# A hybrid decoder layer on one core: the first norm's squares in blocks of four, its factor applied per row block, small constants and two modulation chunks loaded later

## The chip, the cores and the metric

The kernel runs on one core of a Trainium2 chip. The metric is device time in microseconds (us) of one execution; of before there are three runs with a median of 1945.05 us (1939.61 to 1948.28). A separate profiled execution took 1943.4 us, and its trace spans 1941.6 us.

## The reference, cut to what matters

One layer over 256 tokens of width 2048, in float32: an adaLN modulation, a norm, one input projection for attention (NSA) and retention, an output projection, then a second norm with a retrieval among 16384 experts, and a last norm. The change touches only the start:

```python
c_act = jax.nn.silu(c)
mod = (c_act @ w_ada[l] + b_ada[l]).reshape(B, 6, 1, D)
shift1, scale1, gate1, shift2, scale2, gate2 = jnp.moveaxis(mod, 1, 0)
h = rmsnorm(x, g_norm_mix[l]) * (1.0 + scale1) + shift1
q_a, k_c, v_c, k_s, v_s, k_w, v_w, g_a, q_r, k_r, v_r, g_r = split_cols(h @ w_in[l], IN_SIZES)
```

`rmsnorm` divides each token by the root of its mean square (plus 1e-6) and multiplies by a gain per feature.

## The kernel before, in words

Features lie on partitions in 16 row blocks of 128, tokens (256) along the free axis: `xT` is 128x16x256. Weights arrive in chunks of 128x2048 f32 (1.05 MB) through a ring of four `raw` tiles, by SP's queue, in program order. A weight chunk is split in two parts, `whi` by a cast on ACT (L156) and `wlo` by a subtraction on DVE (L157); each has two tiles. TensorE multiplies them with the two parts `hh` and `hl` of the normed input (together the tile `act`), in three products (hi with hh, hi with hl, lo with hh).

The modulation w_ada is 96 chunks `adaT` (j, k): part j of six, row block k. Each is one multiply-and-sum over 128x2048 on DVE (L197) against silu(c), the tile `crow`. The first 32, shift (j = 0) and scale (j = 1), are needed by row blocks 0 to 15; the others are worked off in the background until the output projection. The function `background` takes as many as a pace per stage says, and `row_in(k)` first takes those that row block k needs. The stages at the front are

- the norm: 16 squares on ACT (L249), a running sum on DVE (L253), a sum over partitions by TensorE, the power -0.5 on POOL (`pow_mhalf`, L219), a diagonal and a matmul that spread it as a row (`rrow`), and four multiplications of `xT` by it (L298);
- A: row blocks 0 to 7 of the input, 2048 columns, 16 column blocks in 8 PSUM banks `bkA`. Per row block: load and split `winA`, scale and shift `xT` (L293), cast it (`hh`, L294), subtract (`hl`, L295), two background chunks, then 48 matmuls;
- C: the same row blocks, 1024 further columns, 4 chunks, banks `bkC`;
- B: all 16 row blocks, 1664 columns, banks `bkB`, `bvB`, `bgB`; row blocks 8 to 15 are modulated here. In this text "row 14" and "row 15" are its last two;
- D and NSA: 12 chunks `winD` over row blocks 8 to 15 (`psD`), mixed with the attention. D0 is the first of them, D1 the second. The compressed keys need `kT2`, which four POOL DMAs turn from `kcv`, and tables `nal` (16 of 192 KB, four tiles) and `csm`, `small`.

A list scheduler puts the instructions of each engine in order by program position, so the order on an engine is not the order in the code. An engine runs its list strictly in that order.

Of the kernel before, what the change touches and what calls it, by code (L numbers as in the profile page):

```python
# [20 lines left out]
P = 128  # L21
# [93 lines left out]
def body(ctx, tc, a, out, dbg=None, stop=None):  # L115
# [130 lines left out]

    def sumsq(wpool, kb, acc, src, tag="pr"):
        sq = wpool.tile([P, S], F32, name="sq", tag=tag, bufs=3)
        nc.scalar.activation(sq, src, AF.Square)  # L249
        if kb == 0:  # L250
            nc.vector.tensor_copy(acc, sq)
        else:
            nc.vector.tensor_add(acc, acc, sq)  # L253

    def row_rstd(pool, wpool, accs, tags, ident, copy=True):

        ps = [pool.tile([P, 2], F32, name="psq", tag=t) for t in tags]
        for i, acc in enumerate(accs):
            for tt in range(2):
                nc.tensor.matmul(ps[tt][:, 0:1], acc[:, tt * P:(tt + 1) * P], ones[:, 0:1], start=i == 0, stop=i == len(accs) - 1)  # L260
        rc = wpool.tile([P, 2], F32, name="rcol")
        for tt in range(2):
            nc.vector.tensor_scalar(rc[:, tt:tt + 1], ps[tt][:, 0:1], 1.0 / D, EPS, op0=OP.mult, op1=OP.add)
        pow_mhalf(rc, rc, 2)
        dg = wpool.tile([P, S], F32, name="rdiag", tag="pr", bufs=3)
        for tt in range(2):
            nc.vector.tensor_scalar(dg[:, tt * P:(tt + 1) * P], ident, rc[:, tt:tt + 1], None, op0=OP.mult)
        ps = pool.tile([P, S], F32, name="psr", tag=tags[0])
        nc.tensor.matmul(ps, ones, dg, start=True, stop=True)
        if not copy:  # L270
            return ps
        r = wpool.tile([P, S], F32, name="rrow")
        nc.scalar.copy(r, ps)
        return r


    with ExitStack() as fctx:
# [3 lines left out]
        nc.vector.memset(ones, 1.0)  # L281
        small = fp.tile([P, 128 + 480 + 30], F32, name="small")
        nc.gpsimd.dma_start(small, a["small"][:, 0:638])
        ident = small[:, 0:128]
        ncmp = small[:, 128:608].rearrange("p (t h n) -> p t h n", t=2, h=HEADS)
        cval = small[:, 608:638].rearrange("p (t n) -> p t n", t=2)
        csm = fp.tile([P, 160], F32, name="csm")
        nc.gpsimd.dma_start(csm, a["csm"])

        def modulate(k, e, t, gi, sh, hh, hl):  # L290

            for i in range(k, e):
                nc.scalar.activation(t[:, i - k, :], t[:, i - k, :], AF.Identity, bias=modc[:, sh, i:i + 1], scale=scol[:, gi, i:i + 1])  # L293
            nc.scalar.copy(hh[:, k:e, :], t)  # L294
            nc.vector.tensor_sub(hl[:, k:e, :], t, hh[:, k:e, :].bitcast(F32))  # L295

        def normalise(dst, src, rrow):
            nc.vector.tensor_mul(dst, src, rrow[:, None, :].to_broadcast([P, dst.shape[1], S]))  # L298

# [8 lines left out]
        pp = fctx.enter_context(tc.tile_pool(name="fpsum", bufs=2, space=PS))  # L308
        banks = lambda name, shape, tags: [pp.tile(shape, F32, name=f"{name}{i}", tag=t) for i, t in enumerate(tags)]
        crow = c_row(fp, pp)  # L310
        for q in range(4):
            nc.sync.dma_start(xT[:, 4 * q:4 * q + 4, :], a["xT"][:, 4 * q:4 * q + 4, :])
        acc = fp.tile([P, S], F32, name="sqacc")
        for k in range(KB):
            sumsq(fp, k, acc, xT[:, k, :])
        rrow = row_rstd(pp, fp, [acc], ["S", "S"], ident)
        for k in range(0, KB, 4):
            normalise(xT[:, k:k + 4, :], xT[:, k:k + 4, :], rrow)

# [4 lines left out]
        def background(n=1):  # L324
            credit[0] += PACE[n] if isinstance(n, str) else n
            n = int(credit[0] + 1e-6)
            credit[0] -= n
            for _ in range(n):
                if not todo:
                    return  # L330
                j, k = todo.pop(0)
                ada_chunk(j, k, crow)
                if j == 0:
                    nc.vector.tensor_add(modc[:, 0:2, k], modc[:, 0:2, k], b_col[:, 0:2, k])
                    nc.vector.tensor_scalar(scol[:, 0, k:k + 1], modc[:, 1, k:k + 1], 1.0, g_mix[:, k:k + 1],
                                            op0=OP.add, op1=OP.mult)
# [9 lines left out]

        def rows_T(bank, b, hi, lo, col, k, k0, k1, first=True):
            w = slice(col, col + P)
            for n, (x, y) in enumerate(((hi, hh), (hi, hl), (lo, hh))):
                nc.tensor.matmul(bank[:, b, :], x[:, w], y[:, k, :], start=k == k0 and n == 0 and first,  # L350
# [7 lines left out]
        def row_in(k):  # L358
            while len(todo) > 96 - 2 * (k + 1):
                background(1)  # L360
            modulate(k, k + 1, xT[:, k:k + 1, :], 0, 0, hh, hl)

# [9 lines left out]
        for k in range(KH):  # L372
            hi, lo = win_row(a["winA"], k, 2048)
            row_in(k)
            background("A")
            for b in range(16):
                rows_T(bk[b // 2], b % 2, hi, lo, b * P, k, 0, KH, b % 2 == 0)
        wait_in(oT, bk)
        bk = banks("bkC", [P, 2, S], "AASS")
        for q in range(KH // 2):  # L380
# [134 lines left out]
        for gp in range(2):  # L515
# [3 lines left out]
            for r in range(4):  # L519
# [5 lines left out]
                for hf in range(2):  # L525
# [776 lines left out]
```

## Time and profile before

| what | before |
|---|---|
| median of the runs | 1945.05 us |
| profiled execution, its span | 1943.4 us, 1941.6 us |
| TensorE busy | 1826.8 us, 94% of the span |
| DVE busy | 1479.4 us, 76% |
| DMA | 651.86 MB, mean 336 GB/s |

A share of busy time is a mean over stages with different limits. What a change at the front is worth has to be read from the stretch it touches, and from what TensorE does right behind it.

### The profile page before, as it was taken

To read this page: it belongs to the slowest core of one execution; us is meant where nothing else is said; L and a number is where in the kernel's file an instruction comes from. 1 tells how busy PE (TensorE), PEld (TensorE's weight loads), DVE (VectorE), ACT (ScalarE), POOL (GpSimd) and SP (SyncE) were. 2 spreads that over 40 slices of the span, in tenths; PEclk is the share of its full clock that TensorE was granted. 3 is DMA by queue.
4 is the path that set the end of the run, shared out by engine and by line. 5 is a ranking of instruction groups with operands and counts; after the bars stand their busy time and mean duration, and the time that the engine had idled before them with its cause. 6 is when DMAs were issued, how large, how long until landed. Compare 5 with 4: busy or idle time off the path is not lost.

```text
span 1941.6 us, 28423 instructions
## 1 busy us (share of the span) xinstructions
PE 1826.8 (94%) x11302; PEld 1594.3 (82%) x11302; DVE 1479.4 (76%) x2247; ACT 699.4 (36%) x1192; POOL 348.6 (18%) x254
## 2 busy tenths in 40 slices
PE   5899899999987999989999999999999999999995
PEld 4798778788766899989997767779999998777773
DVE  7877888889985898487578888874455557899875
ACT  3444353635434421021134444451111114555552
POOL 1000001011010012102123323221111212344210
PEclk9999998989988999999999999999999999999998
DMA  8989888989993589989989999989999989999981
GB/s 341 381 310 358 324 303 271 346 287 377 374 321 134 185 297 386 424 319 376 361 357 402 348 382 372 340 307 375 397 357 360 361 303 376 383 394 383 388 323 44
DMA packets 94312, 651.86 MB, mean 336 GB/s; under 512 B 11410, under 2 KB 11586, under 8 KB 18402
## 3 DMA queue, kind: packets, MB, share of 16 engines
q1 hardware_dynamic: 66818, 467.78, 63.6%
q0 software_dynamic: 27360, 182.26, 24.2%
q8 instruction: 89, 1.46, 0.3%
q14 instruction: 45, 0.36, 0.0%
HBM read 643.92 MB, written 4.21 MB: 334 GB/s over the span
## 4 chain that ended last, share of the span: by engine, by line
PE 73%; DVE 11%; DMA 6%; issue 6%; ACT 3%; POOL 0%; SPq 0%; ACTq 0%; POOLq 0%; DVEq 0%
PE acc L960 30%; PE psU L1058 27%; PE psN L449 4%; DVE wlo L157 3%; DMA raw<-in_adaT 2%; DVE raw L197 2%; PE psA L235 2%; PE psD L350 2%; ACT whi L156 2%; PE pg L1043 1%; DMA raw<-in_winA 1%; PE psA L236 1%; PE bkB L350 1%; DMA x2d<-xT 1%; PE bkC L350 1%
## 5 line engine op out<-in xcount | busy, mean ns | idle before, releaser
L157 DVE TENSOR_TENSOR wlo<-raw,whi 128x2048 fp32r<-128x2048 f32 (+2 forms) x215 | 479.3, 2239 | 139.3 <-ACT whi L156 90.0
L1058 PE MATMUL psU<-xT,raw 128*128 128x160 f32 x4096 | 570.8, 301 | 5.8 <-ACT ge L1063 4.5
L1058 PEld LDWEIGHTS psU<-xT,raw 128*128 128x128 f32 x4096 | 560.2, 191 | 6.5 <-ACT ge L1063 4.6
L156 ACT CAST whi<-raw 128x2048 fp32r<-128x2048 f32 (+2 forms) x215 | 400.7, 1869 | 228.0 <-PE psA L235 40.7
L960 PE MATMUL acc<-whi,cc 128*128 128x512 f32 x1512 | 376.3, 396 | 16.7 <-ACT whi L156 16.7
L960 PEld LDWEIGHTS acc<-whi,cc 128*128 128x128 f32 x1512 | 286.6, 190 | 89.4 <-ACT whi L156 19.8
L960 PE MATMUL acc<-wlo,cc 128*128 128x512 f32 x1008 | 257.1, 395 | 2.3 <-DVE wlo L157 2.3
L197 DVE SCALAR_TENSOR_TENSOR raw<-raw,crow 128x2048 f32<-128x2048 f32 x96 | 219.3, 2286 | 21.5 <-DMA raw<-in_adaT 21.4
L960 PEld LDWEIGHTS acc<-wlo,cc 128*128 128x128 f32 x1008 | 164.6, 164 | 66.9 <-DVE wlo L157 5.1
L449 PE MATMUL psN<-whi,act 128*128 128x512 f32 x512 | 166.1, 400 | 2.3 <-ACT sg L628 2.3
L1064 DVE TENSOR_TENSOR X<-X,ge 128x160 f32<-128x160 f32 (+19 forms) x94 | 26.0, 278 | 156.2 <-ACT ge L1063 146.6
L1060 ACT ACTIVATE X<-psU 128x160 f32<-128x160 f32 (+19 forms) x102 | 25.6, 252 | 330.8 <-PE psU L1058 330.7
L449 PEld LDWEIGHTS psN<-whi,act 128*128 128x128 f32 x512 | 95.9, 188 | 25.0 <-ACT sg L628 2.7
L936 ACT CAST cc<-X 128x192 fp32r<-128x192 f32 x128 | 44.8, 353 | 197.1 <-PE acc L960 197.1
L449 PE MATMUL psN<-wlo,act 128*128 128x512 f32 x256 | 103.3, 404 | 3.0 <-DVE wlo L157 2.9
L235 PE MATMUL psA<-act,whi 128*128 128x512 f32 x240 | 87.4, 405 | 8.6 <-ACT whi L156 8.6
L800 POOL DMA_INDIRECT rows<-in_urow,sx x32 | 59.8, 1869 | 130.1 <-DVE rows L841 100.5
L350 PE MATMUL psD<-act,whi 128*128 128x256 f32 x384 | 76.3, 298 | 3.6 <-ACT whi L156 3.6
L800 POOL DMA_INDIRECT xT<-in_v,sx x21 | 57.3, 2727 | 119.6 <-DVE cc L937 76.6
L800 POOL DMA_INDIRECT s<-in_urow,sx x26 | 47.1, 1811 | 145.7 <-DVE s L841 111.6
L841 DVE SCALAR_TENSOR_TENSOR rows<-rows,h2t 128x2048 f32<-128x2048 f32 x32 | 73.0, 2284 | 0.0
L350 PEld LDWEIGHTS psD<-act,whi 128*128 128x128 f32 x384 | 63.2, 201 | 6.4 <-ACT whi L156 4.0
(339 smaller groups left out, 2406.8 us busy)
## 6 DMA issues: line engine op xcount, KB each, us to landing
raw<-in_u SPq DMA_DIRECT2D x128, 1024.0 KB
raw<-in_v SPq DMA_DIRECT2D x128, 1024.0 KB
raw<-in_adaT SPq DMA_DIRECT2D x96, 1024.0 KB
raw<-in_winN SPq DMA_DIRECT2D x16, 1024.0 KB
raw<-in_woutN SPq DMA_DIRECT2D x16, 1024.0 KB
raw<-in_wqT SPq DMA_DIRECT2D x16, 1024.0 KB
raw<-in_winB SPq DMA_DIRECT2D x16, 832.0 KB
raw<-in_winD SPq DMA_DIRECT2D x12, 1024.0 KB
```

The costliest lines, as they stand in the source:

```text
L156: nc.scalar.copy(hi[:, sl], r[:, sl])
L157: nc.vector.tensor_sub(lo[:, sl], r[:, sl], hi[:, sl].bitcast(F32))
L197: nc.vector.scalar_tensor_tensor(r, r, 1.0, crow, op0=OP.mult, op1=OP.mult, accum_out=modc[:, j, k:k + 1])
L235: nc.tensor.matmul(p_, hi[:, sl], act[:, k], start=k == 0, stop=False, skip_group_check=True)
L350: nc.tensor.matmul(bank[:, b, :], x[:, w], y[:, k, :], start=k == k0 and n == 0 and first, stop=k == k1 - 1 and n == 2, skip_group_check=True)
L449: nc.tensor.matmul(ps[tt], x[:, k, ts_], y[:, w], start=k == 0 and j == 0, stop=k == KB - 1 and j == 2)
L800: pin(nc.gpsimd.indirect_dma_start(out=r, out_offset=None, in_=src, in_offset=bass.IndirectOffsetOnAxis(ap=o, axis=0)))
L841: pin(nc.vector.scalar_tensor_tensor(r, r, 1.0, h, op0=OP.mult, op1=OP.mult, accum_out=d[:, e:e + 1]))
L936: nc.scalar.copy(ch, xb(j))
L960: nc.tensor.matmul(acc[c][0:m], x, w[:, c[1] * 512:(c[1] + 1) * 512], start=jj == 0 and n == 0, stop=jj == HALF - 1 and n == 2 - c[0], ski ...
L1058: nc.tensor.matmul(ps, w[:, k * P:(k + 1) * P], xT[:, k, 0:TU], start=k == 0, stop=k == KB - 1)
L1064: nc.vector.tensor_mul(xb(j)[:, 0:done], xb(j)[:, 0:done], ge[:, 0:done])
```

## The change

The squares are taken over four row blocks at once (128x1024), the running sum is folded on DVE in the end, and the 1/D with 1e-6, the diagonal and the copy of the norm move from DVE to ACT; all of this has a raised priority. `xT` is no longer multiplied by `rrow` in four wide steps: per row block one DVE instruction multiplies by scale and `rrow`, ACT adds the shift while it casts to `hh`, and a second DVE instruction makes `hl`. The bias of the shift is added on POOL, one instruction per row block; 1 + b_ada is made once. Only `ident` is loaded at the start; `csm` and the rest of `small` go on SP's queue after stage A's last `winA`, and the `nal` loads of POOL's queue behind the `kT2` turns. In stage A the matmuls run product by product over all 16 column blocks, and the last row block takes no background chunks. B's `bv` and `bg` swap bank tags, and D0's load and split are issued ahead of the copies of B's banks.

```diff
-    def sumsq(wpool, kb, acc, src, tag="pr"):
-    def row_rstd(pool, wpool, accs, tags, ident, copy=True):
...
-        small = fp.tile([P, 128 + 480 + 30], F32, name="small")
-        nc.gpsimd.dma_start(small, a["small"][:, 0:638])
+        ident = fp.tile([P, P], F32, name="ident")
+        nc.gpsimd.dma_start(ident, a["small"][:, 0:128])
...
-        nc.gpsimd.dma_start(csm, a["csm"])
-
-        def modulate(k, e, t, gi, sh, hh, hl):
-
-            for i in range(k, e):
-                nc.scalar.activation(t[:, i - k, :], t[:, i - k, :], AF.Identity, bias=modc[:, sh, i:i + 1], scale=scol[:, gi, i:i + 1])
-            nc.scalar.copy(hh[:, k:e, :], t)
-            nc.vector.tensor_sub(hl[:, k:e, :], t, hh[:, k:e, :].bitcast(F32))
-
-        def normalise(dst, src, rrow):
-            nc.vector.tensor_mul(dst, src, rrow[:, None, :].to_broadcast([P, dst.shape[1], S]))
+        def modulate(k):
+
+            t, shift = xT[:, k, :], modc[:, 0, k:k + 1]
+            nc.vector.scalar_tensor_tensor(t, t, scol[:, 0, k:k + 1], rrow, op0=OP.mult, op1=OP.mult)
+            nc.scalar.activation(hh[:, k, :], t, AF.Identity, bias=shift)
+            nc.vector.scalar_tensor_tensor(hl[:, k, :], t, shift, hh[:, k, :].bitcast(F32), op0=OP.add, op1=OP.subtract)
...
-        acc = fp.tile([P, S], F32, name="sqacc")
-        for k in range(KB):
-            sumsq(fp, k, acc, xT[:, k, :])
-        rrow = row_rstd(pp, fp, [acc], ["S", "S"], ident)
-        for k in range(0, KB, 4):
-            normalise(xT[:, k:k + 4, :], xT[:, k:k + 4, :], rrow)
+        with tc.high_priority(offset=200):
+            for q in range(4):
+                sq = acc if q == 0 else sqs[(q + 1) % 2]
+                nc.scalar.activation(sq, xT[:, 4 * q:4 * q + 4, :], AF.Square)
+                if q in (1, 2):
+                    nc.vector.tensor_add(acc, acc, sq)
+                if q > 1:
+                    fold(acc if q == 2 else sq)
+                    by_token(acc if q == 2 else sq, q == 2)
+            rc = fp.tile([P, 2], F32, name="rcol")
+            for tt in range(2):
+                nc.scalar.activation(rc[:, tt:tt + 1], psq[tt][:, 0:1], AF.Identity, bias=eps, scale=1.0 / D)
+            pow_mhalf(rc, rc, 2)
+            dg = fp.tile([P, S], F32, name="rdiag", tag="pr", bufs=3)
+            for tt in range(2):
+                nc.scalar.activation(dg[:, tt * P:(tt + 1) * P], ident, AF.Copy, scale=rc[:, tt:tt + 1])
+            psr = pp.tile([P, S], F32, name="psr", tag="S")
+            nc.tensor.matmul(psr, ones, dg, start=True, stop=True)
+            nc.scalar.copy(rrow, psr)
...
                 if j == 0:
-                    nc.vector.tensor_add(modc[:, 0:2, k], modc[:, 0:2, k], b_col[:, 0:2, k])
-                    nc.vector.tensor_scalar(scol[:, 0, k:k + 1], modc[:, 1, k:k + 1], 1.0, g_mix[:, k:k + 1],
+                    nc.gpsimd.tensor_add(modc[:, 0, k:k + 1], modc[:, 0, k:k + 1], b_col[:, 0, k:k + 1])
+                elif j == 1:
+                    nc.vector.tensor_scalar(scol[:, 0, k:k + 1], modc[:, 1, k:k + 1], b1[:, k:k + 1], g_mix[:, k:k + 1],
...
             row_in(k)
-            background("A")
-            for b in range(16):
-                rows_T(bk[b // 2], b % 2, hi, lo, b * P, k, 0, KH, b % 2 == 0)
+            if k < KH - 1:
+                background("A")
+            for n in range(3):
+                for b in range(16):
+                    rows_T(bk[b // 2], b % 2, hi, lo, b * P, k, 0, KH, b % 2 == 0, (n,))
         wait_in(oT, bk)
+        for dst, src in ((csm, a["csm"]), (small, a["small"][:, 128:638])):
+            tc.keep_in_program_order(nc.sync.dma_start(dst, src))
...
-        bv = banks("bvB", [P, 512], "AA")
-        bg, = banks("bgB", [P, 1, S], "S")
+        bv = banks("bvB", [P, 512], "SS")
+        bg, = banks("bgB", [P, 1, S], "A")
...
+        d_split = lambda i: split(load(a["winD"][i].rearrange("p k b e -> p (k b e)")))
+        d_next = d_split(0)
...
-                    nc.gpsimd.dma_start(nal, a["nali"][h])
+                    with tc.issue_after(turned.ins):
+                        nc.gpsimd.dma_start(nal, a["nali"][h])
```

The order on DVE at the start of the program, before, from the last squares on (`sq` and `sqacc` are the squares and their sum; `raw_182`, `raw_185` the first two modulation chunks):

```order
L197 SCALAR_TENSOR_TENSOR raw_182,modc_65<-raw_182,crow_95 128x2048
L253 TENSOR_TENSOR sqacc_114<-sqacc_114,sq_157 128x256
L253 TENSOR_TENSOR sqacc_114<-sqacc_114,sq_160 128x256
L197 SCALAR_TENSOR_TENSOR raw_185,modc_65<-raw_185,crow_95 128x2048
L263 TENSOR_SCALAR rcol_167<-psq_163 128x1
```

and now, from the first sum on (`raw_148`, `raw_152` are the same two chunks):

```order
L303 TENSOR_TENSOR sqacc_118<-sqacc_118,sq_119 128x1024
L303 TENSOR_TENSOR sqacc_118<-sqacc_118,sq_120 128x1024
L289 TENSOR_TENSOR sqacc_118<-sqacc_118 128x512
L289 TENSOR_TENSOR sq_119<-sq_119 128x512
L290 TENSOR_TENSOR sqacc_118<-sqacc_118 128x256
L290 TENSOR_TENSOR sq_119<-sq_119 128x256
L199 SCALAR_TENSOR_TENSOR raw_148,modc_67<-raw_148,crow_99 128x2048
L334 TENSOR_SCALAR scol_68<-modc_67,b1_97,cols_58 128x1
L199 SCALAR_TENSOR_TENSOR raw_152,modc_67<-raw_152,crow_99 128x2048
L265 SCALAR_TENSOR_TENSOR xT_60<-xT_60,scol_68,rrow_123 128x256
L267 SCALAR_TENSOR_TENSOR act_72<-xT_60,modc_67,act_72 128x256
```

All sums of squares now stand ahead of the first modulation chunk, and the first row block is ready after one 128x256 product in place of a pass over `xT`.

The order on DVE at the end of stage B, before: `wlo_1575` is row 14, `wlo_1622` row 15; `raw_1581` is the shift chunk of row block 15.

```order
L157 TENSOR_TENSOR wlo_1575<-raw_1572,whi_1574 128x1664
L197 SCALAR_TENSOR_TENSOR raw_1581,modc_65<-raw_1581,crow_95 128x2048
L334 TENSOR_TENSOR modc_65<-modc_65,cols_58 128x2
L335 TENSOR_SCALAR scol_66<-modc_65,cols_58 128x1
L157 TENSOR_TENSOR wlo_1622<-raw_1619,whi_1621 128x1664
L295 TENSOR_TENSOR act_70<-xT_60,act_70 128x256
L407 COPY ksw0_84<-bkB2_960 128x256
```

and now, with `wlo_1536` row 14, `wlo_1586` row 15, `wlo_1632` D0; `raw_1539` the shift chunk of row block 14, `raw_1546` and `raw_1589` the scale and shift chunks of row block 15:

```order
L157 TENSOR_TENSOR wlo_1536<-raw_1533,whi_1535 128x1664
L199 SCALAR_TENSOR_TENSOR raw_1539,modc_67<-raw_1539,crow_99 128x2048
L199 SCALAR_TENSOR_TENSOR raw_1546,modc_67<-raw_1546,crow_99 128x2048
L267 SCALAR_TENSOR_TENSOR act_72<-xT_60,modc_67,act_72 128x256
L334 TENSOR_SCALAR scol_68<-modc_67,b1_97,cols_58 128x1
L265 SCALAR_TENSOR_TENSOR xT_60<-xT_60,scol_68,rrow_123 128x256
L157 TENSOR_TENSOR wlo_1586<-raw_1583,whi_1585 128x1664
L199 SCALAR_TENSOR_TENSOR raw_1589,modc_67<-raw_1589,crow_99 128x2048
L157 TENSOR_TENSOR wlo_1632<-raw_1629,whi_1631 128x2048
```

Three modulation chunks stand between row 14's and D0's subtraction, where one stood between row 14's and row 15's; the `hl` of row 15 and the copies follow only behind D0's subtraction. On ACT D0's cast likewise stands ahead of row 15's `hh` (the row `act_72`):

```order
L156 CAST whi_1585<-raw_1583 128x1664
L156 CAST whi_1631<-raw_1629 128x2048
L266 ACTIVATE act_72<-xT_60,modc_67 128x256
L412 COPY kcv_85<-bkB0_918 128x256 x2
L412 COPY kcv_85<-bkB1_919 128x256 x2
```

Before, row 15's cast, its scale and shift and its `hh` were followed by the copies, and D0's cast came behind these.

## Rows read from the trace of the kernel before

**Rows 1.** The page: TensorE over the whole span.
```profile
PE 1826.8 (94%) x11302; PEld 1594.3 (82%) x11302; DVE 1479.4 (76%) x2247; ACT 699.4 (36%) x1192; POOL 348.6 (18%) x254
```
**Rows 2.** Windows: stretch, length, busy us of each engine; granted clock, DMA share, GB/s.
```profile
30.00:40.00 10.00, 7.04 (x41) 6.84 (x42) 10.00 (x11) 1.20 (x3) 0.00 (x0) 1.00 0.76 283
70.00:80.00 10.00, 6.22 (x50) 6.01 (x51) 9.01 (x12) 2.82 (x3) 0.00 (x0) 1.00 1.01 383
...
170.00:180.00 10.00, 10.00 (x74) 9.43 (x74) 8.52 (x10) 2.94 (x4) 0.00 (x0) 1.00 0.97 372
190.00:200.00 10.00, 4.73 (x28) 3.94 (x28) 6.22 (x9) 5.63 (x9) 2.50 (x4) 0.83 0.76 241
```
**Rows 3.** Timeline of the start: start, duration, instruction, idle before and releaser.
```profile
4.39 2.15 POOL L530 DMA_DIRECT2D nal<-in_nali  x4
...
13.01 1.33 ACT L249 ACTIVATE sq<-xT 128x256 f32<-128x256 f32 x4 [0.78 <-DMA xT<-in_xT]
...
20.59 1.90 ACT L156 CAST whi<-raw 128x2048 fp32r<-128x2048 f32 x1 [6.25 <-DMA raw<-in_winA]
...
24.74 4.62 DVE L298 TENSOR_TENSOR xT<-xT,rrow 128x1024 f32<-128x1024 f32 x4
...
27.08 2.07 PE L350 MATMUL bkA<-act,whi 128*128 128x256 f32 x8 [3.27 <-ACT act L294]
```
**Rows 4.** Timeline of DVE, end of stage A (row block 7).
```profile
83.40 2.29 DVE L157 TENSOR_TENSOR wlo<-raw,whi 128x2048 fp32r<-128x2048 f32 x1 [1.08 <-ACT whi L156]
85.61 2.29 DVE L197 SCALAR_TENSOR_TENSOR raw<-raw,crow 128x2048 f32<-128x2048 f32 x1
...
87.82 0.42 DVE L295 TENSOR_TENSOR act<-xT,act 128x256 fp32r<-128x256 f32 x1
```
**Rows 5.** Timeline of ACT, stage A and the last rows of B.
```profile
81.47 1.90 ACT L156 CAST whi<-raw 128x2048 fp32r<-128x2048 f32 x1 [5.74 <-DMA raw<-in_winA]
83.28 0.60 ACT L293 ACTIVATE xT<-xT,modc,scol 128x256 f32<-128x256 f32 x1
89.19 0.59 ACT L368 COPY oT<-bkA 128x512 f32<-128x512 f32 x1 [4.88 <-PE bkA L350]
...
194.57 1.89 ACT L156 CAST whi<-raw 128x2048 fp32r<-128x2048 f32 x1
```
**Rows 6.** Timeline of TensorE, from stage A to stage C.
```profile
88.30 0.39 PE L350 MATMUL bkA<-act,whi 128*128 128x256 f32 x1 [1.10 <-DVE act L295]
...
93.01 0.28 PE L350 MATMUL bkA<-act,wlo 128*128 128x256 f32 x1
93.14 1.10 PE L350 MATMUL bkC<-act,whi 128*128 128x256 f32 x8
95.09 0.39 PE L350 MATMUL bkC<-act,wlo 128*128 128x256 f32 x1 [0.85 <-DVE wlo L157]
```
**Rows 7.** Chain that ended last, last rows of B to D1: start, length, what.
```profile
172.40 7.86 DMA raw<-in_winB
...
181.95 1.89 DVE wlo L157
183.84 2.22 DVE raw L197 x2
...
187.62 0.74 PE bkB L350 x4
...
191.77 0.24 PE bvB L402
...
208.53 0.03 DVE wlo L157
```
**Rows 8.** The power -0.5 on POOL: count, duration ns min/median/max, first and last start.
```profile
L219 POOL TENSOR_TENSOR brs<-brs,mhalf x8: 693/846/2731, 427.7 to 481.3; 128x2 f32<-128x2 f32 x8
L219 POOL TENSOR_TENSOR msn<-msn,mhalf x2: 4599/4754/4909, 326.7 to 423.2; 128x16 f32<-128x16 f32 x2
...
L219 POOL TENSOR_TENSOR rcol<-rcol,mhalf x1: 715/715/715, 21.3 to 21.3; 128x2 f32<-128x2 f32 x1
```

More of the change, by code (lines that the diff above doesn't have):

```diff
@@ L175, in body @@
     nc.gpsimd.memset(mhalf, -0.5)
+    eps = base.tile([P, 1], F32, name="eps")
+    nc.gpsimd.memset(eps, EPS)
     modc = base.tile([P, 6, KB], F32, name="modc")
@@ L245, in summed @@
         nc.vector.tensor_add(dst, dst, ps[:, 0, 0:n])
-    def sumsq(wpool, kb, acc, src, tag="pr"):
[L248 to L253, printed above, removed]
-    def row_rstd(pool, wpool, accs, tags, ident, copy=True):
[L257 to L274, printed above, removed]
     with ExitStack() as fctx:
@@ L281, in body @@
         nc.vector.memset(ones, 1.0)
-        small = fp.tile([P, 128 + 480 + 30], F32, name="small")
-        nc.gpsimd.dma_start(small, a["small"][:, 0:638])
-        ident = small[:, 0:128]
-        ncmp = small[:, 128:608].rearrange("p (t h n) -> p t h n", t=2, h=HEADS)
-        cval = small[:, 608:638].rearrange("p (t n) -> p t n", t=2)
-        csm = fp.tile([P, 160], F32, name="csm")
-        nc.gpsimd.dma_start(csm, a["csm"])
-        def modulate(k, e, t, gi, sh, hh, hl):
-            for i in range(k, e):
-                nc.scalar.activation(t[:, i - k, :], t[:, i - k, :], AF.Identity, bias=modc[:, sh, i:i + 1], scale=scol[:, gi, i:i + 1])
-            nc.scalar.copy(hh[:, k:e, :], t)
-            nc.vector.tensor_sub(hl[:, k:e, :], t, hh[:, k:e, :].bitcast(F32))
-        def normalise(dst, src, rrow):
-            nc.vector.tensor_mul(dst, src, rrow[:, None, :].to_broadcast([P, dst.shape[1], S]))
+        ident = fp.tile([P, P], F32, name="ident")
+        nc.gpsimd.dma_start(ident, a["small"][:, 0:128])
+        small = fp.tile([P, 480 + 30], F32, name="small")
+        ncmp = small[:, 0:480].rearrange("p (t h n) -> p t h n", t=2, h=HEADS)
+        cval = small[:, 480:510].rearrange("p (t n) -> p t n", t=2)
+        csm = fp.tile([P, 160], F32, name="csm")
+        def modulate(k):
[3 more added lines that the diff above has]
+            nc.vector.scalar_tensor_tensor(hl[:, k, :], t, shift, hh[:, k, :].bitcast(F32), op0=OP.add, op1=OP.subtract)
         kcv = fp.tile([P, 4, 2, P], F32, name="kcv", tag="f4k", bufs=2)
@@ L309, in body @@
         banks = lambda name, shape, tags: [pp.tile(shape, F32, name=f"{name}{i}", tag=t) for i, t in enumerate(tags)]
+        b1 = fp.tile([P, KB], F32, name="b1")
+        nc.vector.tensor_scalar(b1, b_col[:, 1, :], 1.0, None, op0=OP.add)
         crow = c_row(fp, pp)
@@ L312, in body, with fold, by_token @@
             nc.sync.dma_start(xT[:, 4 * q:4 * q + 4, :], a["xT"][:, 4 * q:4 * q + 4, :])
-        acc = fp.tile([P, S], F32, name="sqacc")
-        for k in range(KB):
-            sumsq(fp, k, acc, xT[:, k, :])
-        rrow = row_rstd(pp, fp, [acc], ["S", "S"], ident)
-        for k in range(0, KB, 4):
-            normalise(xT[:, k:k + 4, :], xT[:, k:k + 4, :], rrow)
+        acc = fp.tile([P, 4, S], F32, name="sqacc", tag="blk", bufs=1)
+        sqs = [fp.tile([P, 4, S], F32, name="sq", tag="f4k", bufs=2) for _ in range(2)]
+        psq = [pp.tile([P, 2], F32, name="psq", tag="S") for _ in range(2)]
+        def fold(t):
+            nc.vector.tensor_add(t[:, 0:2, :], t[:, 0:2, :], t[:, 2:4, :])
+            nc.vector.tensor_add(t[:, 0, :], t[:, 0, :], t[:, 1, :])
+        def by_token(t, first):
+            for tt in range(2):
+                nc.tensor.matmul(psq[tt][:, 0:1], t[:, 0, tt * P:(tt + 1) * P], ones[:, 0:1], start=first, stop=not first)
+        rrow = fp.tile([P, S], F32, name="rrow")
+        with tc.high_priority(offset=200):
[12 more added lines that the diff above has]
+            dg = fp.tile([P, S], F32, name="rdiag", tag="pr", bufs=3)
+            for tt in range(2):
+                nc.scalar.activation(dg[:, tt * P:(tt + 1) * P], ident, AF.Copy, scale=rc[:, tt:tt + 1])
+            psr = pp.tile([P, S], F32, name="psr", tag="S")
+            nc.tensor.matmul(psr, ones, dg, start=True, stop=True)
+            nc.scalar.copy(rrow, psr)
         todo = [(j, k) for k in range(KB) for j in (1, 0)] + [(j, k) for j in (2, 3, 4, 5) for k in range(KB)]
@@ L345, in win_row, with rows_T @@
             return split(r, n)
-        def rows_T(bank, b, hi, lo, col, k, k0, k1, first=True):
+        def rows_T(bank, b, hi, lo, col, k, k0, k1, first=True, ns=range(3)):
             w = slice(col, col + P)
-            for n, (x, y) in enumerate(((hi, hh), (hi, hl), (lo, hh))):
+            for n in ns:
+                x, y = ((hi, hh), (hi, hl), (lo, hh))[n]
                 nc.tensor.matmul(bank[:, b, :], x[:, w], y[:, k, :], start=k == k0 and n == 0 and first,
@@ L360, in row_in @@
                 background(1)
-            modulate(k, k + 1, xT[:, k:k + 1, :], 0, 0, hh, hl)
+            modulate(k)
         def wait_in(dst, bk):
@@ L413, in body @@
             for hf in range(2):
-                nc.gpsimd.dma_start(kT2[j * 64:(j + 1) * 64, :, hf, :], kcv[hf * 64:(hf + 1) * 64, :, j, :])
+                turned = nc.gpsimd.dma_start(kT2[j * 64:(j + 1) * 64, :, hf, :], kcv[hf * 64:(hf + 1) * 64, :, j, :])
         def d_pair(i):
-            hi, lo = split(load(a["winD"][i].rearrange("p k b e -> p (k b e)")))
+            hi, lo = d_split(i) if i else d_next
             bk = pp.tile([P, 2, S], F32, name="psD", tag="A")
```

## The prediction, made before the change was run

> **What bounds the kernel now.** I read the page first: TensorE is busy for 94% of the span [rows 1], so a change at the front is worth what it takes out of TensorE's waiting there, and it stays gained only where TensorE runs without a gap behind it. The windows come next. From 70 to 80 us TensorE is busy for 6.22 of 10 us while the DMA engines are busy all the time at 383 GB/s: stage A is fed too slowly. From 30 to 40 us the DMA moved only 283 GB/s, DVE being busy without a gap. From 170 to 180 us, in stage B, TensorE is full at 10.00 us, with the DMA nearly full too (0.97, 372 GB/s). From 190 to 200 us it has 4.73 us of work: that is the handover from B to D [rows 2]. Then the timelines. The first wide matmul begins at 27.08 us, behind a norm whose last piece of input came at 13.01 us, a weight cast that waited 6.25 us for its DMA, and 4.62 us of multiplying the whole of xT [rows 3]. At the end of A the cast waits 5.74 us for winA [rows 5], and the hl of row block 7 stands behind a modulation chunk of 2.29 us [rows 4]. TensorE waits for that hl, and once more 0.85 us for C's first wlo [rows 6]. Last, the chain through B's end: it runs over DMA, DVE and TensorE in turn, so there all three are about equally late [rows 7].
>
> **The opening: stage A ends earlier.** Five terms.
>
> Bytes: the four nal loads that were issued at 4.39 us [rows 3] (4 x 128 x 384 f32, 0.79 MB), 510 columns of small (0.26 MB) and csm (0.08 MB) no longer go ahead of the first weights. 1.13 MB at 383 GB/s is 3.0 us. csm and small come back behind the last winA, where they delay only winC, by 0.9 us, and TensorE is then still at row block 7. The bound from below is 0, if those bytes had gone beside other loads at no cost.
>
> The gap: 283 in place of 383 GB/s over 10 us is 2.6 us of lost transfer [rows 2]. It came from ring tiles given back late, with DVE behind. DVE now has 3 wide sums of squares and folds before the first chunk in place of 15 narrow ones around it, and does not do the 4.62 us pass over xT in one go; 8 of the 16 products come only in stage B. I take 2.0 us, between 0 and 2.6. The first matmul itself should move by about 4 us, to 23; that is no term of its own, because A is fed by the DMA.
>
> The chunk: row block 7 takes none, so hl stands right behind wlo: 87.82 less 85.61, 2.2 us [rows 4].
>
> The order of products: before, 4.8 us of matmuls were left when hl came (88.30 to 93.14); now a third of the 48 are done by then, and 32 at 0.12 us (93.01 to 93.14) are 3.8 us: 1.0 us gained [rows 6].
>
> From A to C: before, 8 matmuls of C ran (0.95 us) and then 0.85 us were lost, so C is in effect 1.0 us behind A's end. Now all banks end within the last product. ACT has C's second cast (1.90 us) ahead of the first copy (0.59 us) [rows 5]; that cast can start when the second product is through, 1.9 us before the end, so C starts 0.6 to 0.8 us after A: 0.3 us gained.
>
> Sum 3.0 + 2.0 + 2.2 + 1.0 + 0.3 = 8.5 us, with ends at 3.5 (the last three) and 9.1. The added ACT work (two 128x1 steps, two diagonals, one table load) lies where ACT waited 6.25 us for a weight. The rest of C and of B up to row 13 I cost at nothing: TensorE is full there and shifts as it is.
>
> **The handover from B to D: some of it is given back.** The two chunks left out of A are made up at the end of B. Before, one chunk stood behind row 14's wlo, the shift of row block 15. wlo ends at 183.84, the sum at 186.06, row 15 starts at 187.62 and ends at 192.01, 4.4 us of matmuls [rows 7]; row 14 so began at about 183.2. Now, on the same clock, the shift of row block 14 stands behind row 14's wlo: 183.84 + 2.22, then the add on POOL (0.72, [rows 8]) and the hh on ACT (0.60, [rows 5]), so row 14 starts at 187.4, 4.2 us late, and ends at 191.8. D0's cast stands ahead of row 15's hh on ACT and needs the whi tile of row 14: 191.8 + 1.89 + 0.60 is 194.3. DVE's D0 subtraction follows the cast (2.29, to 196.0), and row 15's hl that (0.42, to 196.4). TensorE fills part of this with 25 of D0's 48 matmuls (3.0 us); row 15 ends at about 201.7, 9.7 us later than it would have. In exchange D0 is nearly through, while before its cast only began at 194.57 [rows 5].
>
> What counts is D1. Before, its subtraction began at 208.53, 16.5 us after row 15 [rows 7]. If only D0's cast and subtraction (4.2 us) go from that stretch, D1 comes at 201.7 + 12.3 = 214.0, 5.5 us late; if D0's 5.7 us of matmuls go too, at 208.3, 0.2 us early. I take 3.5 late, nearer the first end, because D1's load waits for a ring tile and for DVE, not for TensorE. The other bound above is 10, with the adds on POOL at their slowest (below). The late nal loads fall into a stretch with the DMA at 0.76 [rows 2], and nobody reads them before D1; cost nothing, up to 2 us if they delay D1's load.
>
> **The sum.** 8.5 gained and 3.5 given back is 5.0 us. The profiled execution took 1943.4, so 1938.4 by its clock; the median of the runs stands 1.65 above it, which makes 1940. The stages behind, where the scheduler has reordered details, get 0 with 2 us either way.
>
> **Rivals.** Handover kept free: the DMA has a lead in stage C, since two chunks are gone, and if some of it lasts through B, row 14's weights and shift come before their turn. Then the 5.27 us in which TensorE has nothing from 190 to 200 us [rows 2] shrink by most, since D0 is ready: 8.5 + 4 gained, 1933. For it speaks that D0's split is ahead of the copies; against it that the DMA is at 0.97 before the handover, and the chain goes through a winB load of 7.86 us [rows 7].
>
> POOL waits for DVE: rows 8 show a power on two numbers per partition at 0.715 us with DVE idle, but up to 2.731 us in stretches with wide DVE work, and 4.6 to 4.9 us for 16 numbers. If the power at the start and the two last adds behave so, the opening loses 2.0 us (6.5 left) and each add 2.0 to 2.3, and the handover costs 3.5 + 4.3. Net 1 us lost to 1 gained: 1945. The Trainium skill states such a rule, in "SBUF — State Buffer", section "Who interferes with whom": a DVE instruction with two SBUF inputs and a GpSimd instruction that reads SBUF exclude each other for a whole instruction. By that rule, this rival's time is the likely one; the trace agrees only in part, since the median of the eight powers is 0.846 us.
>
> Slower: row 15 becomes a chain. Place: ACT and DVE at the end of B, where D0's split stands ahead of row 15's hh and hl. If winD0 comes late, because three chunks and a winB are queued ahead of it, row 15 waits for a load it doesn't need, then kcv, kT2 and D1 wait for row 15. Price: the handover at its upper bound of 10, plus a load (1.05 MB at 372 GB/s, 2.8 us) and its sum (2.3), 15 us against 8.5: 1952. It decides from 8.5 us of handover loss on. Against it: winD0 needs only a tile that the shift chunk of row 14 frees.
>
> **How the numbers follow.** Forecast 0.42 (own range 1936 to 1944), handover free 0.28, POOL 0.20, slower 0.10. The range 1929 to 1950 leaves out the far half of the slower case and the best fifth of the free handover. A measurement of this kernel can tell about 0.5%, 9.7 us, from no change. Faster by that is below 1935.3: three quarters of the free handover and a fifth of the forecast, 0.30. Slower by that is above 1954.8, a third of the last case and a little of the others: 0.06. Within it: 0.64.
>
> **What would show it.** Right: the first wide matmul at 22 to 24 us; C's matmuls from about 86; the DMA at over 0.9 from 30 to 40; row 14 waiting for ACT's hh, and TensorE with D0 matmuls inside row 15; D1's subtraction 4 to 6 us earlier than 208.53. Wrong: C from 90 or later (the bytes or the gap were no terms), a handover in which row 14 does not wait (the free case), POOL's adds at 2 us and more (the second rival), or a gain at D1 that is gone by 700 us.

## The result, and the profile after

The changed kernel takes 1958.71 us (median of 5 runs, 1957.01 to 1960.93) against 1944.48 for the kernel before: ratio 1.0071, 95% interval 1.0047 to 1.0095. It is 14 us slower; the forecast was 1940.0, and the range ended at 1950. The profiled execution has a span of 1959.2 us (before 1941.6).

The page and windows of the changed kernel, in the columns of [rows 1, 2]:

```profile
PE 1837.8 (94%) x11306; PEld 1601.3 (82%) x11306; DVE 1480.5 (76%) x2230; ACT 690.1 (35%) x1167; POOL 352.8 (18%) x270
```
```profile
30.00:40.00 10.00, 7.99 (x64) 7.68 (x64) 9.76 (x10) 2.60 (x3) 0.19 (x1) 1.00 1.00 368
70.00:80.00 10.00, 7.05 (x57) 6.56 (x56) 9.30 (x13) 3.08 (x4) 0.43 (x2) 1.00 1.00 392
...
170.00:180.00 10.00, 6.33 (x40) 5.14 (x38) 9.11 (x8) 2.78 (x3) 0.00 (x0) 0.96 0.99 379
180.00:190.00 10.00, 6.15 (x33) 5.48 (x33) 7.63 (x10) 2.90 (x3) 2.37 (x2) 0.70 0.97 376
190.00:200.00 10.00, 8.84 (x67) 8.19 (x68) 4.92 (x5) 4.03 (x9) 1.85 (x3) 1.00 0.71 247
300.00:320.00 20.00, 20.00 (x83) 16.96 (x83) 14.60 (x36) 6.11 (x17) 0.54 (x1) 0.52 0.81 313
440.00:470.00 30.00, 28.30 (x188) 25.46 (x188) 30.00 (x44) 14.37 (x20) 10.30 (x6) 1.00 0.98 372
470.00:500.00 30.00, 28.43 (x136) 23.27 (x135) 28.26 (x53) 18.08 (x25) 6.56 (x4) 1.00 0.95 355
500.00:530.00 30.00, 26.89 (x113) 21.24 (x112) 25.76 (x22) 11.53 (x15) 1.16 (x2) 0.94 0.96 365
```
The same stretches of the kernel before that were not shown yet:
```profile
180.00:190.00 10.00, 9.50 (x67) 8.62 (x66) 7.30 (x9) 4.19 (x4) 0.00 (x0) 1.00 0.96 351
300.00:320.00 20.00, 20.00 (x111) 17.25 (x112) 14.04 (x24) 6.22 (x12) 0.54 (x1) 0.77 0.81 313
440.00:470.00 30.00, 29.98 (x169) 25.69 (x168) 29.59 (x53) 17.90 (x24) 5.58 (x5) 1.00 0.98 384
470.00:500.00 30.00, 30.00 (x137) 24.20 (x136) 28.35 (x41) 16.39 (x21) 3.53 (x3) 1.00 0.98 365
500.00:530.00 30.00, 29.62 (x126) 23.19 (x125) 26.73 (x22) 12.00 (x13) 2.13 (x4) 1.00 1.00 372
```
The front is better fed (DMA 1.00 in place of 0.76 from 30 to 40 us). From 170 to 190 us TensorE is idle for 7.5 us (before 0.5), and about 2 us more go to its clock (0.70 granted from 180 to 190). From 300 to 320 us it is as busy as before, but at a mean granted clock of 0.52 in place of 0.77, so nearly all the time at the lower of its two levels (1.2 GHz): 9.6 us of clock lost in place of 4.6. From 440 to 530 us it is idle for 6.4 us and loses 1.6 to the clock, 8.0 in all; before it was 0.4.

How far each place stands from the kernel before is read best from one kind of event that all kernels share in the same number: the weight subtractions wlo on DVE. The start of the n-th, before, and the distance to it (profiled executions; the right-hand columns are the experiments o6, c1, n_two and y7 below):

| wlo of | before, us | changed | o6: changed, old order to the end | c1: before, x3's order | n_two: two loads | y7: fastest |
|---|---|---|---|---|---|---|
| row 4 of A | 58.53 | -4.8 | -4.3 | -0.5 | -1.2 | -4.5 |
| row 12 of B | 170.48 | -6.8 | -5.9 | +0.3 | +0.5 | -9.4 |
| row 15 of B | 186.41 | -2.0 | -2.5 | -1.1 | -0.4 | -10.4 |
| D0 | 196.49 | -5.5 | -4.9 | -0.3 | -0.1 | -10.6 |
| D1 | 208.53 | +0.6 | +3.3 | +2.7 | +0.1 | -9.8 |
| 37th | 275.01 | +0.3 | +1.8 | +1.2 | -1.0 | -10.9 |
| 54th | 450.38 | +10.8 | +4.8 | -4.2 | +1.1 | -11.5 |
| 71st | 552.37 | +14.1 | +3.8 | +8.0 | +11.4 | -10.4 |
| 96th | 1024.88 | +15.8 | +8.0 | +11.3 | +14.7 | -7.8 |

So there are two losses. The handover gives back the opening's whole gain (-6.8 to +0.6). Then 14 us more go between 275 and 552 us, where the change edits nothing but when the nal loads are issued. In this one profile 10.5 of them stand ahead of the 54th subtraction, and the clock alone accounts for about 7 of those: between the 37th and the 54th it took 18.8 us, before 11.9. Whether that comes again, the experiments have to tell.

The opening went much as forecast. Timeline of ACT and TensorE, changed kernel:
```profile
11.22 1.06 ACT L301 ACTIVATE sq<-xT 128x1024 f32<-128x1024 f32 x1
...
20.32 1.88 ACT L156 CAST whi<-raw 128x2048 fp32r<-128x2048 f32 x1
22.26 5.49 PE L350 MATMUL bkA<-act,whi 128*128 128x256 f32 x32 [3.37 <-ACT whi L156]
...
86.78 0.40 PE L350 MATMUL bkC<-act,whi 128*128 128x256 f32 x2
```
The first wide matmul is at 22.26 (27.08 before, [rows 3]) and stage C begins at 86.78 (93.14, [rows 6]): 6.4 us gained.

The handover, in the chain of waits of the changed kernel (start, length, what):
```profile
177.95 2.22 DVE raw L199 x2
180.17 0.07 issue
180.23 2.19 POOL modc L332
182.42 0.02 issue
182.44 0.52 ACT act L266
...
183.00 1.22 PE bkB L350 x4
...
189.08 1.91 ACT whi L156
...
191.01 2.30 DVE wlo L157
...
193.35 2.67 PE psD L350 x21
196.03 1.71 PE bkB L350 x15
...
197.77 0.04 DVE ksw L413
...
198.52 1.02 DVE raw L199
...
200.76 6.33 DMA raw<-in_winD
...
209.10 2.29 DVE wlo L157
```
Row 14 waits for its forced chunk (177.95), then for POOL's add, and begins at 183.00. TensorE had waited 6.45 us for it, its clock fell meanwhile, and the row takes 6.1 us (to 189.06). D0's cast and 21 of its matmuls stand ahead of row 15, whose matmuls for the ksw banks end at 197.74 (its last one at 198.99). Only then can DVE do the ksw copies, and the chunk behind them (198.52) gives back the ring tile into which D1's weights are loaded, at 200.76. The same load in the chain of the kernel before:
```profile
201.02 5.50 DMA raw<-in_winD
```
So the end of the handover did not move at all.

POOL's 16 adds, count, shortest, median and longest ns:
```profile
L332 POOL TENSOR_TENSOR modc<-modc,cols x16: 191/192/2175, 18.9 to 188.6; 128x1 f32<-128x1 f32 x16
```
The longest is the one in the chain. It starts while DVE is in its next wide sum (180.07 to 182.36) and ends with it; 13 of the 16 took 0.19 to 0.26 us, and the other two (1.77 us each) began during a subtraction on DVE. The rule of the Trainium skill weighed in the prediction ("SBUF — State Buffer", "Who interferes with whom") agrees with these rows.

### The profile page after: what moved, and what is told of

Its sections match the earlier page's. It is cut to its first block, busy times and chain, and to the rows that moved or that the text cites. A ratio compares the mean times of both kernels' runs of the same rounds, so it can differ in the third digit from the quotient of the medians.

```text
span 1959.2 us, 28404 instructions
## 1 busy us (share of the span) xinstructions
PE 1837.8 (94%) x11306; PEld 1601.3 (82%) x11306; DVE 1480.5 (76%) x2230; ACT 690.1 (35%) x1167; POOL 352.8 (18%) x270
## 4 chain that ended last, share of the span: by engine, by line
PE 75%; DVE 11%; DMA 5%; issue 5%; ACT 3%; POOL 1%; ACTq 0%; POOLq 0%; SPq 0%; DVEq 0%
PE acc L967 30%; PE psU L1065 26%; PE psN L455 6%; DVE wlo L157 3%; ACT whi L156 2%; DVE raw L199 2%; PE psA L237 2%; PE psD L350 2%; PE bkC L350 1%; DMA raw<-in_winA 1%; DMA raw<-in_adaT 1%; PE pg L1050 1%; PE psA L238 1%; DMA x2d<-xT 1%; PE sc L542 1%
## 5 line engine op out<-in xcount | busy, mean ns | idle before, releaser
L238 PE MATMUL psA<-act,wlo 128*128 128x256 f32 x240 | 68.4, 286 | 0.5 <-DVE wlo L157 0.5
```

The source lines that it names most:

```text
L238: nc.tensor.matmul(p_[:, 1, :], lo[:, sl], hh[:, k, :], start=False, stop=k == KB - 1, skip_group_check=True)
```

## The experiments

Theory H: the handover loses the gain. Theory O: the loss lies in the order of issue. (Each expectation names its other rivals, S, P, R and T, where it uses them.) The program is written once, and a scheduler, which simulates it, decides what each engine issues next; the diff shows nothing of that behind D0. Behind the gate (psg, the first step after B) 1108 of 1759 TensorE places up to the end of the output projection hold another instruction than before.

**Parts of the handover undone.** Edits to the changed kernel:
```
x1, x3, x6   hi, lo = d_split(i)              # D0 split where it was
x2, x3, x6   background("A")                  # at every row of A again
x6           nc.vector.tensor_add(modc[...])  # in place of nc.gpsimd
```


> The changed kernel with D0's split back inside d_pair(0), behind the copies of B. Theory H (the handover from B to D lost what the opening gained): ACT's D0 cast no longer stands ahead of row 15's hh, so row 15 begins about 3.5 us earlier, the ksw copies and the chunk that gives back D1's tile follow, and D1's subtraction comes 2 to 3 us before 209.10; time 1955 to 1957. Theory O (the loss lies behind 290 us, in the order that the scheduler wrote for the attention stage, where TensorE runs at 1.2 GHz for longer): D1 may move, but the time goes by the length of the stretches at the lower clock: it differs from 1958.7 only if these 20 us (299 to 320) and 15 us (400 to 415) get shorter.

> The changed kernel with the two modulation chunks fetched at the last row of A again; D0's split stays early. H: no forced chunks in front of rows 14 and 15, so row 14 waits neither for a chunk (2.3) nor for POOL's add behind the next one (2.2): D1's subtraction at 204 to 205, A ends about 2.2 us later than in the changed kernel; time 1952 to 1955. O: as for the kernel with the late split, the time goes by the stretches at the lower clock alone, 1944 to 1959, and D1's place says nothing of it.

> Both undone: chunks at the last row of A, D0's split behind the copies; the norm, the constants, the product order, the late nal loads and POOL's adds stay. H: the handover is that of before, shifted by the opening's 6 to 7 us, so D1's subtraction is at 201 to 203 and the time 1937 to 1939. O: D1 at 201 to 203 too, but 1944 or more if the low-clock stretches at 290 to 320 and 390 to 420 sum to more than the 6.8 + 5.1 us of clock loss of before.

> As the kernel with both undone, and the add of b_ada to the shift column on DVE in place of POOL; its order on the engines is nearly that of the kernel with both undone, so it is compared with that. Theory P (POOL's one-column add waits for a wide DVE instruction, 1.8 to 2.2 us where two chunks follow each other): up to 2 us faster than with both undone, where a row waits for it. H: within 1 us of it, since without forced chunks no row waits for the add.

Measured, median and ratio to before (which was run again beside each group, with medians from 1945.5 to 1947.2): x1 1960.99 (1.0071, 1.0046 to 1.0096); x2 1953.74 (1.0036, 1.0021 to 1.0052); x3 1961.83 (1.0088, 1.0065 to 1.0111); x6 1960.88 (1.0070, 1.0043 to 1.0097). H asked for 1937 to 1939 in x3 and falls as the main cause: with the old handover the kernel is no faster than the changed one. D1 in x3 is at 208.44, not at 201 to 203. x1's D1 came later (213.11) where H had it earlier. x2's time lies in H's range, its D1 at 208.00 does not. x6 against x3, in the same order up to the end of the output projection (behind it 113 of 6060 TensorE places differ): no difference that can be told.

**The order held.** From the gate on, each engine's instructions are chained in the order that the scheduler gave them in another kernel; nothing else is edited:
```
+ for x, y in zip(row, row[1:]):   # row: one engine's instructions, in the wanted order
+     tc.add_manual_dep(y, x.name, <order only, no wait>, reason="order")
y2 also:  PACE = dict(A=2, C=1, ...)   # was C=0.5: the two late chunks come in C
          hi, lo = d_split(i)
```


> The changed kernel, but from the gate of the attention stage to the end of the output projection (about 190 to 550 us) every engine is made to issue its instructions in the order that they had in the kernel before; the code that is computed is the same. Theory O (the order that the scheduler wrote is the loss): the front stays, D1's subtraction at about 209, and behind it the distance to before stays at 0 to 3 us instead of growing to 15; time 1944 to 1948. Theory S (the change itself slows these stages: the late nal loads, the adds on POOL, the missing lead): the order does not matter, 1955 to 1960.

> The kernel with both undone (chunks on time, D0's split late), with before's order of issue in the same stretch. O: D1 at 206 to 208, 0 to 2 us earlier than before, and this distance lasts; time 1942 to 1945 in place of 1961.8. S: 1958 to 1962, as without the old order.

> The kernel before, with the order of issue that the kernel with both undone has in the same stretch (the converse). O: the front of before, and then the loss of that kernel behind D1, 10 us: 1952 to 1957. S: nothing of the change is in it, so 1943 to 1946.

> The changed kernel with its two left-out chunks made up in stage C (one chunk per load of C in place of a half), D0's split behind the copies as before, and before's order of issue from the gate on. O with H: no row waits for a forced chunk, so B keeps the opening's 6 to 7 us; D1's subtraction at 202 to 205 and the time 1937 to 1941. If C can't take two more chunks (DVE or DMA full there), rows 8 to 12 come later by up to 4.6 us and it is 1942 to 1945. S: 1950 or more.

o1 1957.45 (1.0050, 1.0032 to 1.0068), o3 1949.74 (1.0019, 0.9995 to 1.0043), c1 1962.47 (1.0087, 1.0063 to 1.0111), y2 1944.98 (0.9990, 0.9973 to 1.0007). c1 decides: the kernel before, every line of it, with x3's order, is 16 us slower; and x3 with the old one is 12 us faster. c1 and o3 both lie 5 us above the range that O gave, and y2 lies in the one for the case that stage C can't take the chunks, not in O's first. o1 was a miss: its profile loses 2 us from D1 to 552 us (13.5 in the changed kernel), as O said, but its median moved by 1 us; the profile is 6.6 us behind at 1024 us and 14 at the end. The order was held only as far as the output projection. Behind it 113 of 6060 TensorE places in o1 differ from before, in the changed kernel none, and o1 loses 8 us between 1062 and 1187 us. c1 and the two loads below (117 and 113 places) lose 8 us there too, but x3 (113) only 3, as the changed kernel does. So order may cost in that place as well; no run holds it there alone.

**Which edit tips the order.** Single edits to the kernel before, without and with the old order held:
```
n_product, p_product:  for n in range(3):           # product outside,
                           for b in range(16):      # block inside
                               rows_T(..., (n,))
n_two, p_two:  nc.gpsimd.dma_start(small[:, 0:128], a["small"][:, 0:128])
               nc.gpsimd.dma_start(small[:, 128:638], a["small"][:, 128:638])
```


> The kernel before with one edit of the change alone: in stage A each product is done for all 16 blocks before the next one. Its order of issue behind the gate is nearly that of the kernel with both undone (26 of 1759 TensorE places differ). O: the edit gains about 1 us at the end of A, and then the loss of that order comes: 1957 to 1963. A rival R (what an edit costs is what it does in its own place): 1943 to 1946.

> The same single edit, with before's order of issue from the gate to the end of the output projection. O: the loss goes, 1943 to 1947. R: no difference to the single edit without it.

> The kernel before with the load of the constants small issued as two DMAs in place of one, same bytes, same tile; nothing else is edited. 397 of 1759 TensorE places behind the gate come out in another order. O: the time may differ from before by several us either way with nothing done that could cost it: from 1940 to 1960, its loss or gain all between 190 and 560 us. R: within 1 us of before, 1944 to 1948.

> The kernel before with small loaded by two DMAs and before's order from the gate to the end of the output projection. O: all of the 16 us go, 1944 to 1948. R (the second DMA itself costs something): 1950 or more.

Product order alone 1955.89 (1.0052, 1.0034 to 1.0070; 1 us under O's range), with the old order 1942.74 (0.9978, 0.9963 to 0.9993). Two loads alone 1963.38 (1.0076, 1.0060 to 1.0093), with the old order 1944.40 (0.9986, 0.9976 to 0.9997). R falls. A load of 0.3 MB at the start of the program, split in two, makes this kernel 16 us slower, and all of it is gone when the order is kept. O's bounds for it, at most 1960 and the whole loss between 190 and 560 us, were too narrow: its profile is 22 us behind at the end, 11 of it from D1 to 552 us and 8 between 1062 and 1187. Windows of the two kernels with two loads, order as scheduled and old order:
```profile
300.00:320.00 20.00, 19.42 (x149) 18.07 (x148) 18.00 (x22) 8.38 (x10) 0.00 (x0) 1.00 0.95 355
440.00:470.00 30.00, 27.51 (x148) 23.47 (x147) 26.76 (x43) 13.56 (x18) 5.80 (x4) 0.94 0.94 359
470.00:500.00 30.00, 28.44 (x128) 22.85 (x128) 25.02 (x44) 16.08 (x25) 4.95 (x4) 0.94 0.83 305
500.00:530.00 30.00, 26.87 (x109) 20.91 (x108) 25.85 (x23) 11.73 (x12) 1.14 (x2) 0.94 0.96 370
```
```profile
440.00:470.00 30.00, 30.00 (x185) 26.43 (x184) 29.54 (x51) 14.66 (x21) 7.70 (x5) 1.00 0.98 373
470.00:500.00 30.00, 30.00 (x141) 24.32 (x140) 28.37 (x41) 18.20 (x23) 3.53 (x2) 1.00 0.96 348
500.00:530.00 30.00, 29.63 (x126) 23.05 (x124) 27.24 (x23) 11.63 (x11) 1.67 (x3) 1.00 1.00 382
```
From 440 to 530 us 7.2 us idle and 5.0 lost to the clock, against 0.4. (The stretch from 300 to 320 is no part of this: the order there is still that of the kernel before, up to about 355 us, and one execution had a clock of 0.77, the other of 1.00. The 5 us more that the changed kernel lost there may be scatter.) One piece of it can be read in full. TensorE's order of weight chunks at the output projection (chunk: matmuls; 19 ends the first tile, 20 begins the second):
```
before:   18:22  psT:2  18:2  psT:2  19:24  20:24  21:24
changed:  18:24  psT:2  19:12 psT:2  19:6  20:2  19:4  20:20  19:2  20:2  21:24
```
ACT and TensorE of the changed kernel there, and ACT of the kernel before (513.13 and 496.50 are the casts of chunk 21):
```profile
505.85 0.41 ACT L679 CAST act<-oT 128x256 fp32r<-128x256 f32 x1
513.13 3.70 ACT L156 CAST whi<-raw 128x2048 fp32r<-128x2048 f32 x2 [6.88 <-PE psN L455]
...
515.08 0.74 PE L455 MATMUL psN<-whi,act 128*128 128x512 f32 x2 [1.52 <-ACT whi L156]
517.41 0.80 PE L455 MATMUL psN<-wlo,act 128*128 128x512 f32 x1 [1.59 <-DVE wlo L157]
```
```profile
496.50 1.92 ACT L156 CAST whi<-raw 128x2048 fp32r<-128x2048 f32 x1 [2.75 <-PE psN L449]
...
502.49 1.92 ACT L156 CAST whi<-raw 128x2048 fp32r<-128x2048 f32 x1 [2.12 <-DMA raw<-in_woutN]
508.64 1.91 ACT L156 CAST whi<-raw 128x2048 fp32r<-128x2048 f32 x1 [2.66 <-DMA raw<-in_woutN]
```
The scheduler put matmuls of chunk 20 ahead of the last ones of 19, presumably to fill a wait in its simulation. On the chip chunk 19 then holds its whi tile until its last two matmuls, beside 20's, and there are two such tiles. The cast of 21 waits 6.88 us for TensorE and TensorE then waits 3.1 us for the cast and the subtraction, at a clock of 0.94 over the stretch. Before, the cast of 21 waited 2.75 us for TensorE and the next two for DMA only, and TensorE was idle for just 0.4 us from 440 to 530. All eight other orders (the changed kernel, x1, x2, x3, x6, c1, product order, two loads) have this crossing of 19 and 20; before's order has not.

All twenty profiles together bear O out: from the 54th to the 71st wlo the twelve with before's order take 101 to 105 us, seven of the eight with another order 111 to 118; only the changed kernel itself, at 105, does not stand out there. From the 37th to the 71st the twelve take 271 to 284 us (mean 279), the eight 284 to 291 (mean 287).

**Which part of the handover, with the old order held.** What each has:
```
         chunks            D0's split   add    order held to
y3       made up in C      early        POOL   output projection
y5       forced, 14/15     late         POOL   output projection
y4       made up in C      late         DVE    output projection
y6       made up in C      late         DVE    second norm
```


> The changed kernel with its two chunks made up in stage C and before's order behind the gate; D0's split stays ahead of B's copies, the add on POOL. H1 (the forced chunks cost): no row waits for a chunk, so the early split does no harm: D0's subtraction at 186 to 189, D1's at 201 to 204, time 1943 to 1946. H2 (the early split costs, since row 15's hh and the chunk that gives D1 its tile stand behind it): D1 at 206 to 209 and 1950 to 1957.

> The changed kernel with D0's split back behind the copies and before's order behind the gate; its two chunks are still forced in front of rows 14 and 15. H1: row 15 at 4 us late and D1 at 207 to 210, 1950 to 1957. H2: D1 at 202 to 205, 1943 to 1946.

> The changed kernel with its two chunks made up in stage C, D0's split late, before's order behind the gate, and the add of b_ada to the shift column on DVE in place of POOL. P (POOL's add waits for wide DVE instructions in front of rows 14 and 15, about 2 us): D1's subtraction up to 2 us earlier than with the add on POOL, 1942 to 1944. H: row 15 isn't late there, so the same as with the add on POOL within 1 us, 1944 to 1946.

> As the kernel with chunks in C, D0's split late, DVE's add and before's order behind the gate, with that order kept to the end of the second norm (about 600 us) in place of the end of the output projection. O: the 2 to 3 us that are lost from 552 to 590 us go, 1941 to 1943. S: that loss is the stage's own, 1944 to 1946.

y3 1946.23 (1.0003, 0.9987 to 1.0018), D1 at 198.38; y5 1951.25 (1.0032, 1.0015 to 1.0049), D1 at 211.36; y4 1944.67 (0.9984, 0.9966 to 1.0001), D1 at 200.17, 2.8 us before y2's 203.00; y6 1941.75 (0.9978, 0.9959 to 0.9996). H1 stands: the forced chunks cost, the early split does not (y3's D1 is 4.6 us before y2's). H1's ranges for D1, 201 to 204 and 207 to 210, were missed by 3 and 1 us. The twenty profiles agree: from row 12's wlo to D1's it takes 45.4 to 49.5 us in the five kernels with forced chunks (changed, x1, y5, o1, o6), late split or early, and 36.7 to 40.7 in the fifteen without. P named the right place, but 2.8 us at D1 is hardly more than two executions of one front differ by (o1 209.64, o6 211.81), and the median shows nothing. y6 decides nothing: the order that it holds to the second norm is the one that y4 has there already, and the two programs are the same, instruction by instruction on every engine. What differs between them is scatter.

**The order held to the end of the program.**

> The changed kernel with before's order of issue from the gate of the attention stage to the end of the program. O (the rest is order too): 1948 to 1951, what its profile with the shorter fixed stretch was behind at 550 us, 3 us, and 1 to 3 us more. Rival T (TensorE's waits in the experts' stage vary from run to run whatever the order): 1953 to 1958, as with the shorter stretch.

> The kernel with chunks in C, D0's split late, DVE's add, and before's order from the gate to the end of the program. O: at most 1 us better than with the order to the second norm, 1940 to 1942. T: the same within its scatter, 1940 to 1944.

o6 1948.72 (1.0010, 0.9994 to 1.0026): 10 us of the changed kernel's loss are order; T does not hold for it. y7, the fastest: 1938.31 (0.9964, 0.9945 to 0.9982), faster than both kernels, and 2 us under the ranges of O and T. Its TensorE list is that of y4 and y6, and about 20 places each on DVE and ACT differ, so the three are better read together. DVE at its handover:
```profile
185.85 2.29 DVE L183 TENSOR_TENSOR wlo<-raw,whi 128x2048 fp32r<-128x2048 f32 x1 [0.79 <-ACT whi L182]
188.06 2.29 DVE L225 SCALAR_TENSOR_TENSOR raw<-raw,crow 128x2048 f32<-128x2048 f32 x1
...
198.73 2.29 DVE L183 TENSOR_TENSOR wlo<-raw,whi 128x2048 fp32r<-128x2048 f32 x1 [3.10 <-ACT whi L182]
```
D0 at 185.85, the chunk right behind, D1 at 198.73: in this profile the opening's gain passes the handover whole.

## Why the prediction was wrong, step by step

The 14 us taken apart, by the ratios to before (0.1% is 1.9 us): y7 stands at -0.36%, the opening kept, 7.0 us gained; o6 is 0.46% above y7, the handover with chunks, split and add, 9.0 us; the changed kernel is 0.61% above o6, the order, 11.9 us. Each difference is uncertain by about 5 us, and y7 is the luckiest of three nearly equal programs: by y4 and y6 (-0.16 and -0.22%) the opening is worth 3 to 4 us and the handover 5 to 6.

- **Opening, 8.5 with ends 3.5 and 9.1: right.** 6.4 us at stage C, 6.8 at row 12; 4.8 to 7.1 at stage C in the ten profiles with this opening. Which term took the 2 us too much is not shown. The signs named came true: first matmul 22.26 (22 to 24), DMA 1.00 from 30 to 40, C at 86.78 (about 86).
- **Handover, 3.5 given back: right in its course, mis-sized; measured 7.4,** between the taken bound 5.5 and the outer one of 10 (7.3 to 11.5 in the five profiles with forced chunks). Row 14 waits for hh and D0's matmuls lie inside row 15, as said. The step that failed is "D1's load waits for a ring tile and for DVE, not for TensorE": it does wait for DVE, but DVE's chunk stands behind the ksw copies, which wait for row 15 on TensorE. An in-order queue hands TensorE's delay on. A smaller term was missing: row 14 was priced at 4.4 us of matmuls and took 6.1, at the clock that fell while TensorE waited (0.70 granted from 180 to 190 us). The sign named for D1, 4 to 6 us earlier, did not come (0.6 late). The price of an add on POOL "at their slowest" (2.19) was paid, too, once, where it counted. y3 and y5 show that the two forced chunks are the cause, not the early split.
- **"Handover kept free", 1933, 0.28:** not what the change does, but what two more chunks in stage C do (D1 at 198.38 in y3).
- **Stages behind, "0 with 2 us either way": this is the step that failed.** The order costs 10 to 12 us: the changed kernel against o6, which has the same code. In the profile 13.5 us go from D1 to 552 us, 0.5 in o6; with no handover in play, c1 loses 5.4 there, the product order 8.3 and the two loads 11.3. On average it is about 9 (287 against 279 us above), so some of the 13.5 is scatter of that one execution, its clock most likely. The reordering was seen before the run and called detail; it needed a price of its own, of both signs, for it covers two thirds of TensorE's places in a stretch with only two whi tiles.
- **The slower rival** (a chain at row 15, 1952) had the right sign by the wrong main place.
- **Left open:** why the scheduler's simulated time turns on so little, on which engine the order costs most, and what executions of one kernel differ by: 1930.2 to 1949.4 in y7, with the granted clock between 0.96 and 0.98 in these kernels. Single profiles can't settle 5 us here.

## What to carry to other kernels

Where a scheduler writes the order, compare the order behind an edit before the time: here an edit at 2 us cost 16 us, hundreds of us later. Compare the lists of the two programs of an experiment too: y4 and y6 turned out to be one program. To learn what an edit is worth, hold the order of the untouched stages fixed on both sides; then tune the order as a thing of its own. And moving work "later" is only free where it lands: these two chunks cost nothing that can be seen in stage C, where TensorE was the limit (busy for 19.90 of 20 us in y7), and about 6 us in front of the last rows (y5 against y3).

## What the runs showed of the hardware that was not expected

- The same 128x1 add on POOL takes 0.19 us, or up to 2.175 when it begins during a wide DVE instruction, and then it ends 0.05 us behind that one. The prediction had priced this; it came for one of the two last adds.
- TensorE's clock fell without a stall that the profile shows: 0.52 from 300 to 320 us at a busy share of 1.00, in the attention stage, with no idle time in the 20 us before either. The kernel before had 0.77 there and the kernel with two loads 1.00, in the same order of issue as before.
- One program, two executions: y4 and y6 between their 37th and 54th wlo do 1059 matmuls each, at a mean granted clock of 0.96 and 0.91, and take 172.41 and 179.40 us:
```profile
268.54:440.95 172.41, 163.78 (x1059) 142.81 (x1057) 150.32 (x277) 78.88 (x155) 23.88 (x21) 0.96 0.87 310
266.87:446.27 179.40, 170.76 (x1059) 149.44 (x1057) 150.98 (x277) 78.33 (x155) 23.97 (x21) 0.91 0.83 297
```
